# Query copies written once to DRAM by GpSimd, and loaded by one DMA per four heads

## The chip, the cores and the metric

The kernel runs on one core of one Trainium2 chip. The metric is device time in microseconds (us) of one execution, the median of several runs. Engines are named as in the profile: PE (TensorE matmul), PEld (TensorE weight load), DVE (VectorE), ACT (ScalarE), POOL (GpSimd) and SP (SyncE, whose queue, SPq, issues most DMAs).

## What is computed

Two transformer blocks over 2048 tokens of width 1024, batch 1, float32. The first (sliding-window attention, a gated recurrence, a mixture of experts) is not touched. The second has a chunked attention with relative positions, and beside it a sparse attention whose 256 keys per query are chosen by an index score. The change touches two inputs of that sparse branch, the queries `qb` (8 heads of 64) and the index queries `iq` (8 heads of 32):

```python
def second_block(x, norm_gain, w_in, ...):
    xn = rms_norm(h, norm_gain[layer])
    qa, ka, va, ga, qb, kb, vb, gb, iq, ik, iw, za, zb = jnp.split(xn @ w_in[layer], offsets, axis=-1)
    ya = chunked_relpos_attention(qa, ka, va, rel_bias[layer]) * jax.nn.silu(ga)
    qb, kb, iq, ik = (partial_rope(...) for each)          # 16 of 64 columns turn, 8 of 32 for the index
    yb = dsa_sparse_attention(qb, kb, vb, iq, ik, iw) * jax.nn.silu(gb)
    merged = gate_a * (ya @ w_branch_a) + gate_b * (yb @ w_branch_b)
    return rms_norm(h + merged @ w_out, final_norm_gain)

def one_block(blk):                                        # of dsa_sparse_attention, 128 queries
    logits = jax.nn.relu(jnp.einsum('bqhd,bsd->bqhs', iqb, ik))
    score = jnp.einsum('bqhs,bqh->bqs', logits, iwb)       # then masked by chunk
    _, idx = lax.top_k(score, 256)
    s = jnp.einsum('bqhd,bqkd->bqhk', qb, gather(k, idx)) * scale
    return jnp.einsum('bqhk,bqkd->bqhd', softmax(s), gather(v, idx))
```

## The kernel before

Tokens are cut into 16 blocks of 128. Float32 products are split: an operand is kept as a high and a low part of float32r, and products of parts are summed. For the sparse branch a head's query is needed with its columns repeated down the partitions (twice for `qb`, four times for `iq`), so that one matmul against the keys, which are stored with their high and low parts in different partitions, gives the whole product.

The second block, class `S3`, runs in stages. Each has front lanes, whose steps are asked first, and a back lane called `fill`, a chain of projections that is asked last:

1. Start: the norm of all 16 token blocks (`norm_lane`, for which POOL gathers two expert outputs of a block from DRAM, `cy<-Y`, and adds them, `cx`), and `proj(0, ...)`. Its token-row groups are numbered g: 0 is keys and values of the sparse branch, 1 is `iq`, 2 and 3 are `qb`, 4 and 5 are `va`. A group of one block is 24 matmuls into a `pA` bank.
2. `chunked(0)`: chunked attention (`a_unit`) of the first 8 blocks, and the selection (`sel_unit`) of blocks 2 to 7. The fill is the rest of the first half's projections, then the groups 0 to 5 and the transposed projections of the second half's blocks.
3. `sparse(range(10))`: sparse attention (`b_unit`) of blocks 0 to 9, beside what is left of that fill.
4. `chunked(1)`, with the selection of blocks 10 to 12, and the last projections as fill.
5. `sparse(range(10, 16))` with the output projections (`tail`) as fill.

The order on each engine is fixed when the program is built: lanes are generators, and a step is written when a clock model with a cost for each instruction (`Clock`, `Engine.cost`) says that its operands are near ready. Engines run their lists in order, so a step that is later on the chip than in the model holds what is behind it on its engine. A stage ends, and the next one's steps may be written, when this loop ends, so when no front lane and no spawned step is left (`ev_n` and others are spawned, by the fill too):

```python
while lanes or self.spawned:
```

Path of the queries: `ev_n` lets ACT copy a finished bank into a staging tile `st` (a ring of 3 tiles for all projections), POOL rotates it (`rotate`: six instructions) and stores it to the DRAM tensor `IQ` or `QB` by a DMA from its own queue. Later `turned` loads the queries of a block in two groups of four heads into the tile `x` (`x4`, one buffer): four DMAs on SP's queue per group, each reading one head's columns several times by a stride of zero. PE transposes the four parts, ACT and DVE split the result into `iqs` or `qd`. In all 28 groups of `IQ` and 32 of `QB` are loaded, 240 DMAs.

Of the kernel before, what the change touches and what calls it, by code (L numbers as in the profile page):

```python
# [16 lines left out]
AF = mybir.ActivationFunctionType  # L17
# [5 lines left out]
T = 2048  # L23
# [11 lines left out]
class Clock:  # L35
# [3 lines left out]
    def __init__(self):  # L39
        self.t = dict.fromkeys(("tensor", "vector", "scalar", "gpsimd", "sync", "dma"), 0.0)  # L40
        self.ready, self.last, self.by, self.free = {}, {}, {}, {}
        self.now, self.open = 0.0, set()
# [1084 lines left out]
class P2:  # L1127
# [184 lines left out]
    def put(self, dst, blk, t):  # L1312
        yield from self.b.load(dst[blk * 128:blk * 128 + 128, :], t)
# [544 lines left out]
class S3:  # L1858


    def __init__(self, b, X2, out, comb=None, skip=()):
        self.comb = comb
        self.b, self.nc, self.I, self.X2, self.out = b, b.nc, b.I, X2, out
        nc = b.nc
        dr = lambda n, s: None if n in skip else nc.dram_tensor(n, s, F32).ap()

        self.QA = dr("QA", (4, 4, 64, T))
        self.KA = dr("KA", (2, 4, 128, T))
        self.VA = dr("VA", (T, 1024))
        self.QB = dr("QB", (T, 512))  # L1870
        self.IQ = dr("IQ", (T, 256))
        self.SG = dr("SG", (8, 128, T))
        self.TZ = dr("TZ", (16, 128, T))
        self.YT = dr("YT", (8, 128, T))
        self.KEEP = dr("KEEP", (3, 128, T))
        self.XND = dr("XND", (2, 2, 128, KT, 512))

        self.parts = dr("W2P", (60, 2, 128, 1024))
        self.flags = set()

        self.with_tail = [i for i in range(24) if i % 3 < 2]
        self.exact, self.limit = False, 0
        self.xt = {}
        self.bias, self.stored = {}, set()
        self.BIAS = dr("BIAS", (NTB, 128, T))
# [174 lines left out]
    def ev_n(self, g, blk, ps):  # L2060
        b, nc = self.b, self.nc
        rp = self.rope[:, blk]
        r = slice(blk * 128, blk * 128 + 128)
        if g >= 4:
            v = yield from self.stage([128, 4, 2, 64], F32R)
            p4 = ps[:, 0:256].rearrange("p (h d) -> p h d", h=4)
            yield from b.on("scalar", ps, v)
            nc.scalar.activation(v[:, :, 0], p4, AF.Copy)
            yield 1
            yield from b.on("vector", v)  # L2070
            b.lo(v[:, :, 1], p4, v[:, :, 0])
            b.done(ps)
            yield 1
            yield from self.store(self.VA[r, (g - 4) * 512:(g - 4) * 512 + 512], v, v.rearrange("p h a d -> p (h a d)").bitcast(F32), ("va", blk, g - 4))
        elif g:
            h = 8 if g == 1 else 4
            x = yield from self.stage([128, h, 256 // h])
            yield from b.on("scalar", ps, x)
            nc.scalar.activation(x, ps[:, 0:256].rearrange("p (h d) -> p h d", h=h), AF.Copy)
            b.done(ps)  # L2080
            yield 1
            yield from b.on("gpsimd", x)
            if g == 1:
                self.rotate(x, rp[:, 16:20], rp[:, 20:24], 8, 4)
                dst, key = self.IQ[r, :], ("iq", blk)
            else:
                self.rotate(x, rp[:, 0:8], rp[:, 8:16], 4, 8)
                dst, key = self.QB[r, (g - 2) * 256:(g - 2) * 256 + 256], ("qb", blk, g - 2)
            yield 1
            yield from self.store(dst, x, x.rearrange("p h d -> p (h d)"), key, "gpsimd")  # L2090
        else:
            x = yield from self.stage([128, 424])
            yield from b.on("scalar", ps, x)
            nc.scalar.activation(x[:, 0:160], ps[:, 0:160], AF.Copy)
            nc.scalar.activation(self.iw[:, blk], ps[:, 160:168], AF.Copy, scale=1.0 / 16)
            b.done(ps)
            nc.scalar.activation(self.vbS[:, blk, 0], x[:, 64:128], AF.Copy)
            yield 1
            yield from b.on("vector", x)
            b.lo(self.vbS[:, blk, 1], x[:, 64:128], self.vbS[:, blk, 0])  # L2100
            yield 1
            yield from b.on("gpsimd", x)
            self.rotate(x[:, 0:64].unsqueeze(1), rp[:, 0:8], rp[:, 8:16], 1, 8)
            self.rotate(x[:, 128:160].unsqueeze(1), rp[:, 16:20], rp[:, 20:24], 1, 4)
            xx = x[:, 168:424].rearrange("p (i d) -> p i d", i=2)
            nc.gpsimd.tensor_copy(xx[:, 0].rearrange("p (a d) -> p a d", a=2), x[:, 0:64].unsqueeze(1).to_broadcast([128, 2, 64]))
            nc.gpsimd.tensor_copy(xx[:, 1].rearrange("p (a d) -> p a d", a=4), x[:, 128:160].unsqueeze(1).to_broadcast([128, 4, 32]))
            yield 1
            pt = yield from b.bank("pT")
            yield from b.on("tensor", xx, pt)  # L2110
            for i in range(2):
                nc.tensor.transpose(pt[:, i * 128:i * 128 + 128], xx[:, i], b.ident)
            b.done(x)
            yield 1
            kk, ii = self.kbS[:, r], self.ikS[:, r]
            yield from b.on("scalar", pt)
            nc.scalar.activation(kk, pt[:, 0:128], AF.Copy)
            nc.scalar.activation(ii, pt[:, 128:256], AF.Copy)
            yield 1
            yield from b.on("vector", kk)  # L2120
            b.lo(kk[64:128], pt[64:128, 0:128], kk[64:128])
            b.lo(ii[32:64], pt[32:64, 128:256], ii[32:64])
            b.lo(ii[96:128], pt[96:128, 128:256], ii[96:128])
            b.done(pt)
            self.flags.add(("kb", blk))
            yield 1
# [280 lines left out]
                    yield self.a_unit(p, c, t)  # L2407


    def turned(self, src, n, d, k, put):  # L2410

        b, nc, P = self.b, self.nc, self.P
        for g in range(n // 4):
            x = yield from P.get([128, 4, 128], F32, "x4", bufs=1)
            yield from b.on("sync", x)
            for h in range(4):
                c = (g * 4 + h) * d
                nc.sync.dma_start(x[:, h].rearrange("p (a d) -> p a d", a=k), src[:, c:c + d].unsqueeze(1).to_broadcast([128, k, d]))
            yield 1
            pt = yield from b.bank("pT")  # L2420
            yield from b.on("tensor", x, pt)
            for h in range(4):
                nc.tensor.transpose(pt[:, h * 128:h * 128 + 128], x[:, h], b.ident)
            b.done(x)
            yield 1
            yield from put(g, pt)
            b.done(pt)

    def sel_unit(self, blk):
        b, nc, P = self.b, self.nc, self.P  # L2430
# [11 lines left out]
        iq = yield from P.get([128, 8, 128], F32R, "iqs", bufs=1)  # L2442

        def put(g, pt):
# [5 lines left out]
            yield from b.on("vector", iq)  # L2450
            b.lo(o[64:128], p3[64:128], o[64:128])
            yield 1
        yield from self.turned(self.IQ[blk * 128:blk * 128 + 128, :], 8, 32, 4, put)
        acc = yield from P.get([128, self.NM], F32, "acc", bufs=self.nsel)
        pcs = [(a, min(N, a + 512)) for a in range(0, N, 512)]
        left = [0]
# [1 line left out]
        for j, (a0, a1) in enumerate(pcs):  # L2458
# [4 lines left out]
            for h in range(8):  # L2463
                ps = yield from b.bank("pS")
# [142 lines left out]
    def q_lane(self, blks):  # L2607
        b, nc, P = self.b, self.nc, self.P
        for blk in blks:
            yield from self.wait(("qb", blk, 0), ("qb", blk, 1))  # L2610
            qd = yield from P.get([128, 8, 2, 128], F32R, "qd", bufs=1)

            def put(g, pt):
                o = qd[:, g * 4:g * 4 + 4]
                p3 = pt.rearrange("p (h q) -> p h q", h=4)
                yield from b.on("scalar", pt, qd)
                nc.scalar.activation(o[:, :, 0], p3, AF.Copy)
                yield 1
                yield from b.on("vector", qd)
                b.lo(o[:, :, 1], p3, o[:, :, 0])  # L2620
                yield 1
            yield from self.turned(self.QB[blk * 128:blk * 128 + 128, :], 8, 64, 2, put)
            self.qd[blk] = qd

    def b_unit(self, blk, p):
# [472 lines left out]
```

## Time and profile before

| what | value |
|---|---|
| median of 3 runs (lowest, highest) | 4062.14 us (4050.82, 4066.87) |
| the profiled execution: its time, its span | 4061.26 us, 4059.4 us |
| granted TensorE clock, mean | 0.951 |
| PE, PEld busy | 3646.1 us (90%), 3167.4 us (78%) |
| DVE, ACT, POOL busy | 2734.8, 2283.2, 901.4 us (67, 56, 22%) |
| DMA packets; under 512 B | 425744; 129360 |

A busy time is a sum over the whole span; stages differ much in what limits them. The profiled execution is 0.88 us below the median of the runs.

### The profile page before, as it was taken

The page shows a single profiled execution, that of the slowest core. Times are in us where ns is not written, and L with a number is a line of the kernel's source. Part 1 is how long each engine was busy: PE and PEld are TensorE (multiplying, and loading weights), DVE is VectorE, ACT ScalarE, POOL GpSimd, SP SyncE. Part 2 cuts the span into 40 slices and gives each one's busy share as a digit, 9 for nine tenths or more (in the row PEclk, how much of TensorE's full clock was granted, in tenths as well). Part 3 has the DMA queues.
Part 4 walks back from the last instruction along what each step waited for, and adds up shares of the span by engine and source line. Part 5 has one row for each costly group of instructions (what it writes and reads, how often), then busy time and mean ns, then how long its engine had stood idle before and what let it go on. Part 6 is the DMA issues. An engine that isn't in the chain of part 4 may idle for free.

```text
span 4059.4 us, 64576 instructions
## 1 busy us (share of the span) xinstructions
PE 3646.1 (90%) x21649; PEld 3167.4 (78%) x21649; DVE 2734.8 (67%) x7027; ACT 2283.2 (56%) x4628; POOL 901.4 (22%) x1650
## 2 busy tenths in 40 slices
PE   3999999979969999397999989999889988999997
PEld 2888788768858888296777779888678877999997
DVE  7866785697777777526366743467766656878772
ACT  3654655565546666424257755357667774676751
POOL 1310000031011100473044526111033321211110
PEclk9999999979989999598999989999889998999999
DMA  6233451125358887739887773543166527787767
GB/s 229 79 108 110 137 198 60 64 81 167 130 202 314 314 315 285 263 126 339 290 255 249 249 283 108 169 147 101 43 187 180 173 81 270 259 281 272 265 230 283
DMA packets 425744, 801.28 MB, mean 197 GB/s; under 512 B 129360, under 2 KB 245296, under 8 KB 424496
## 3 DMA queue, kind: packets, MB, share of 16 engines
q1 hardware_dynamic: 407472, 748.70, 54.3%
q0 software_dynamic: 17920, 48.26, 3.5%
q8 instruction: 176, 2.88, 0.3%
q14 instruction: 176, 1.44, 0.1%
HBM read 571.02 MB, written 234.18 MB: 198 GB/s over the span
## 4 chain that ended last, share of the span: by engine, by line
PE 37%; DMA 7%; POOL 4%; DVE 3%; issue 3%; ACT 2%; SPq 1%; POOLq 0%; DVEq 0%; ACTq 0%
PE pA L122 22%; PE pS L122 5%; PE pT L122 5%; PE pU L122 5%; POOL rot L122 1%; DMA x<-IQ 1%; SPq L122 1%; DMA x<-QB 1%; DMA tz<-TZ 1%; POOL st L122 1%; DMA Q<-QA 0%; DMA sg<-SG 0%; DVE scb L122 0%; DVE pp L122 0%; POOL QB L122 0%
## 5 line engine op out<-in xcount | busy, mean ns | idle before, releaser
L122 PE MATMUL pA<-xnl,whi 128*128 128x512 f32 x1024 | 415.3, 406 | 5.4 <-DVE st L122 5.4
L122 DVE TENSOR_TENSOR wlo<-ld,whi 128x1024 fp32r<-128x1024 f32 x271 | 328.7, 1243 | 112.6 <-ACT whi L122 74.8
L122 PE MATMUL pA<-xnh,wlo 128*128 128x512 f32 x1024 | 403.7, 394 | 0.4 <-DVE wlo L122 0.4
L122 PE MATMUL pA<-xnh,whi 128*128 128x512 f32 x1024 | 403.9, 394 | 0.0
L122 DVE TENSOR_TENSOR pp<-pT,pp 128x256 fp32r<-128x256 f32 (+1 forms) x568 | 295.1, 537 | 117.5 <-ACT pp L122 113.8
L122 ACT ACTIVATE pp<-pT 128x256 fp32r<-128x256 f32 (+1 forms) x568 | 260.6, 478 | 201.5 <-PE pT L122 189.3
L122 PE MATMUL pA<-hlo,whi 128*128 128x512 f32 x832 | 352.1, 423 | 10.0 <-issue 6.7
L122 PE MATMUL pA<-hhi,wlo 128*128 128x512 f32 x832 | 328.8, 395 | 0.0
L122 PE MATMUL pA<-hhi,whi 128*128 128x512 f32 x832 | 327.9, 394 | 0.0
L122 ACT ACTIVATE whi<-ld 128x1024 fp32r<-128x1024 f32 x212 | 213.5, 1052 | 59.0 <-PE pA L122 35.3
L122 DVE SCALAR_TENSOR_TENSOR acc<-rl,iw,acc 128x512 f32<-128x512 f32 (+3 forms) x304 | 220.8, 727 | 38.0 <-ACT rl L122 31.4
L122 PEld LDWEIGHTS pA<-xnh,wlo 128*128 128x128 f32 x1024 | 193.9, 189 | 44.8 <-DVE wlo L122 1.1
L122 ACT ACTIVATE bias<-acc,sst 128x1152 f32<-128x1152 f32 (+13 forms) x168 | 220.0, 1309 | 13.3 <-DVE sst L122 9.6
L122 PEld LDWEIGHTS pA<-xnl,whi 128*128 128x128 f32 x1024 | 195.4, 191 | 33.6 <-issue 5.8
L122 PE MATMUL pA<-wlo,xnh 128*128 128x256 f32 (+1 forms) x672 | 200.9, 299 | 22.2 <-DVE st L122 12.4
L122 PEld LDWEIGHTS pA<-xnh,whi 128*128 128x128 f32 x1024 | 194.9, 190 | 29.4
L122 PE MATMUL pU<-pp,vbS 128*128 128x256 f32 x1088 | 203.2, 301 | 10.2 <-DVE pp L122 8.3
L122 ACT ACTIVATE rl<-pS 128x512 f32<-128x512 f32 (+3 forms) x304 | 163.6, 544 | 82.4 <-PE pS L122 42.9
L122 PE MATMUL pA<-whi,xnl 128*128 128x256 f32 (+1 forms) x672 | 197.5, 294 | 4.1 <-DMA xnl<-XND 4.1
L122 PE MATMUL pA<-whi,xnh 128*128 128x256 f32 (+1 forms) x672 | 197.6, 294 | 0.0
L122 ACT ACTIVATE st<-pA 128x256 f32<-128x256 f32 (+4 forms) x160 | 73.6, 460 | 202.6 <-PE pA L122 161.5
L122 PEld LDWEIGHTS pA<-hlo,whi 128*128 128x128 f32 x832 | 159.4, 192 | 35.9 <-issue 9.4
(494 smaller groups left out, 11117.2 us busy)
## 6 DMA issues: line engine op xcount, KB each, us to landing
whi<-W2P SPq DMA_DIRECT2D x172, 512.0 KB
wlo<-W2P SPq DMA_DIRECT2D x172, 512.0 KB
ld<-in_w_gu_dram SPq DMA_DIRECT2D x128, 512.0 KB
ld<-in_w_dn_dram SPq DMA_DIRECT2D x64, 512.0 KB
W2P<-whi SPq DMA_DIRECT2D x57, 512.0 KB
W2P<-wlo SPq DMA_DIRECT2D x57, 512.0 KB
Y<-ym SPq DMA_DIRECT2D x48, 512.0 KB
xl<-in_wadaT_dram SPq DMA_DIRECT2D x32, 512.0 KB
```

Source lines behind the costliest of these rows:

```text
L122: r = real(*a, **k)
```

## The change

The rotated queries get their copy in the staging tile: the tile is now `[128, h, 2, 256 // h]`, POOL copies the rotated half to the other half, and stores twice the width. `QB` and `IQ` have 1024 columns. A row of `QB` holds each head twice, stored by one DMA; a row of `IQ` holds each head four times, stored by two DMAs of the same tile, each in 1024 runs of 256 B. `turned` then loads 512 consecutive columns, that is four heads with all copies, by one DMA. Nothing else is edited.

```diff
-        self.QB = dr("QB", (T, 512))
-        self.IQ = dr("IQ", (T, 256))
+        self.QB = dr("QB", (T, 1024))
+        self.IQ = dr("IQ", (T, 1024))
...
             h = 8 if g == 1 else 4
-            x = yield from self.stage([128, h, 256 // h])
+            x = yield from self.stage([128, h, 2, 256 // h])
+            x0 = x[:, :, 0]
             yield from b.on("scalar", ps, x)
-            nc.scalar.activation(x, ps[:, 0:256].rearrange("p (h d) -> p h d", h=h), AF.Copy)
+            nc.scalar.activation(x0, ps[:, 0:256].rearrange("p (h d) -> p h d", h=h), AF.Copy)
...
-                self.rotate(x, rp[:, 16:20], rp[:, 20:24], 8, 4)
-                dst, key = self.IQ[r, :], ("iq", blk)
+                self.rotate(x0, rp[:, 16:20], rp[:, 20:24], 8, 4)
             else:
-                self.rotate(x, rp[:, 0:8], rp[:, 8:16], 4, 8)
-                dst, key = self.QB[r, (g - 2) * 256:(g - 2) * 256 + 256], ("qb", blk, g - 2)
-            yield 1
-            yield from self.store(dst, x, x.rearrange("p h d -> p (h d)"), key, "gpsimd")
+                self.rotate(x0, rp[:, 0:8], rp[:, 8:16], 4, 8)
+            nc.gpsimd.tensor_copy(x[:, :, 1], x0)
+            yield 1
+            if g == 1:
+                dst = self.IQ[r, :].rearrange("t (h b c) -> t h b c", h=8, b=2)
+                for i in range(2):
+                    yield from b.G("dma_start", dst[:, :, i], x.rearrange("p h a d -> p h (a d)"))
+                b.done(x)
+                self.flags.add(("iq", blk))
+            else:
+                yield from self.store(self.QB[r, (g - 2) * 512:(g - 2) * 512 + 512], x, x.rearrange("p h a d -> p (h a d)"), ("qb", blk, g - 2), "gpsimd")
...
-    def turned(self, src, n, d, k, put):
+    def turned(self, src, put):
...
-        for g in range(n // 4):
+        for g in range(2):
             x = yield from P.get([128, 4, 128], F32, "x4", bufs=1)
-            yield from b.on("sync", x)
-            for h in range(4):
-                c = (g * 4 + h) * d
-                nc.sync.dma_start(x[:, h].rearrange("p (a d) -> p a d", a=k), src[:, c:c + d].unsqueeze(1).to_broadcast([128, k, d]))
-            yield 1
+            yield from b.load(x.rearrange("p h d -> p (h d)"), src[:, g * 512:g * 512 + 512])
```

Since the clock model has a cost for the copies and stores, the built order changes from the first `iq` group on. Three places follow, in the order as built.

On POOL, at the first `iq` groups of the second half's blocks (in stage 2), each tile had its rotation and one store; before:

```order
L122 TENSOR_TENSOR rot<-st_27489,rope 128x32 x4
L122 TENSOR_TENSOR st_27489<-rot 128x8x4 x2
L122 DMA IQ<-st_27489 128x256
L122 TENSOR_TENSOR rot<-st_27543,rope 128x32 x4
L122 TENSOR_TENSOR st_27543<-rot 128x8x4 x2
L122 DMA IQ<-st_27543 128x256
```

And now:

```order
L122 TENSOR_TENSOR rot<-st_27443,rope 128x32 x4
L122 TENSOR_TENSOR st_27443<-rot 128x8x4 x2
L122 COPY st_27443<-st_27443 128x8x32
L122 DMA IQ<-st_27443 1024x1x64
L122 TENSOR_TENSOR rot<-st_27496,rope 128x32 x4
L122 TENSOR_TENSOR st_27496<-rot 128x8x4 x2
L122 COPY st_27496<-st_27496 128x8x32
L122 DMA IQ<-st_27443 1024x1x64
```

Each tile has one copy and one DMA more, and the next tile's rotation stands between its two stores.

On SP, where stage 3 begins (`x<-QB` is its first load, `BIAS<-bias` the last store of stage 2's selection); before:

```order
L122 DMA wlo_27772<-W2P 128x1024
L122 DMA BIAS<-bias_27457 128x1024
L122 DMA x_0_28016<-QB 128x2x64 x4
L122 DMA whi_28095<-W2P 128x1024
L122 DMA wlo_28096<-W2P 128x1024
L122 DMA whi_28101<-W2P 128x1024
L122 DMA wlo_28102<-W2P 128x1024
L122 DMA x_0_28121<-QB 128x2x64 x4
```

And now, nine rows after the store `BIAS<-bias_27640`:

```order
L122 DMA VA<-st_28429 128x512
L122 DMA VA<-st_28457 128x512
L122 DMA VA<-st_28504 128x512
L122 DMA x_0_28532<-QB 128x512
L122 DMA VA<-st_28546 128x512
L122 DMA VA<-st_28581 128x512
L122 DMA x_0_28599<-QB 128x512
```

The four loads are one, and the first load of stage 3 no longer follows that store: eight weight loads and three stores of group 4 (`VA`) have come between. Counted in PE's order, 312 matmuls of the fill (13 row groups of 24) that stood in stage 3 now stand before it. From the last fill matmul of stage 3 to its end there were 410 matmuls, now there are 572. Behind the end of stage 3 PE's two lists are nearly alike.

On POOL in stage 1, at the end of the first half's `qb` groups; before:

```order
L122 TENSOR_TENSOR rot<-st_20690,rope 128x32 x4
L122 TENSOR_TENSOR st_20690<-rot 128x4x8 x2
L122 DMA QB<-st_20690 128x256
L122 DMA cy_2_20297<-Y,pos 128x1024
L122 DMA cy_2_20793<-Y,pos 128x1024
```

And now, with 11 stores of `QB` still to come:

```order
L122 COPY st_20307<-st_20307 128x8x32
L122 DMA cy_2_20310<-Y,pos 128x1024
L122 DMA IQ<-st_20183 1024x1x64
L122 DMA cy_2_20388<-Y,pos 128x1024
L122 DMA IQ<-st_20261 1024x1x64
```

The gathers and the additions of two token blocks (8 and 9) have moved ahead of those stores.

## Rows read from the trace of the kernel before

**Rows 1.** Waits of PE from stage 2 on: us in total, times, longest.

```profile
PE pT L122 <- DMA x<-QB: 30.7, 8, 26.4
...
PE pT L122 <- DMA x<-IQ: 13.1, 17, 2.5
...
PE pS L122 <- DMA x<-IQ: 5.8, 1, 5.8
```

**Rows 2.** Timeline of SP and PE at the start of stage 5.

```profile
3352.22 2.41 SPq L122 DMA_DIRECT2D x<-QB  x4
...
3357.97 1.09 PE L122 MATMUL pT<-ident,x 128*128 128x128 f32 x4 [26.39 <-DMA x<-QB]
```

**Rows 3.** Stretches of stages 1 to 5: us, busy (and count) of each engine, clock, DMA.

```profile
1730.00:1830.00 100.00, 97.54 (x829) 97.33 (x828) 25.84 (x58) 28.62 (x79) 73.46 (x266) 1.00 0.38 133
1830.00:1920.00 90.00, 66.33 (x411) 61.86 (x411) 57.63 (x111) 39.39 (x75) 28.59 (x17) 0.85 0.93 337
...
2010.00:2500.00 490.00, 452.29 (x2492) 385.12 (x2491) 292.66 (x804) 307.98 (x772) 224.33 (x461) 0.97 0.74 238
```

**Rows 4.** Timeline of SP and PE around one `IQ` load (start, us).

```profile
2955.00 3.91 SPq L122 DMA_DIRECT2D x<-IQ  x4
...
2960.68 1.40 PE L122 MATMUL pS<-K,Q 128*128 128x320 f32 x4 [5.80 <-DMA x<-IQ]
...
2962.07 1.44 PE L122 MATMUL pT<-ident,x 128*128 128x128 f32 x4
```

**Rows 5.** Tiles x and IQ: duration ns min/median/max of issuing instructions; then landing.

```profile
L122 SPq DMA_DIRECT2D x<-QB x128: 359/468/1796, 2498.6 to 3869.2; - x128
L122 SPq DMA_DIRECT2D x<-IQ x112: 359/507/4374, 2017.1 to 3636.0; - x112
...
L122 POOL DMA_DIRECT2D IQ<-st x16: 580/580/630, 1726.7 to 2483.0; - x16
...
DMA to landing us min/median/max: 2.0/2.0/4.4
```

**Rows 6.** SP's issues (ns) of 1024 runs of 512 B, and of 128 rows.

```profile
L122 SPq DMA_DIRECT2D XND<-th x8: 519/520/1095, 1860.9 to 1946.0; - x8
L122 SPq DMA_DIRECT2D XND<-tl x8: 513/676/1465, 1866.0 to 1947.4; - x8
...
L122 SPq DMA_DIRECT2D KA<-st x32: 319/358/2719, 1908.9 to 2754.1; - x32
```

**Rows 7.** Timeline of POOL, one `iq` group of the second half, and the next one's begin.

```profile
2478.44 0.83 POOL L122 TENSOR_TENSOR rot<-st,rope 128x32 f32<-128x32 f32 x4 [0.64 <-ACT st L122]
2479.34 0.46 POOL L122 TENSOR_TENSOR st<-rot 128x32 f32<-128x32 f32 x2
2480.10 0.58 POOL L122 DMA_DIRECT2D IQ<-st  x1 [0.30 <-POOL st L122]
2481.32 0.82 POOL L122 TENSOR_TENSOR rot<-st,rope 128x32 f32<-128x32 f32 x4 [0.63 <-ACT st L122]
```

**Rows 8.** Groups by shape on POOL: copies, the gathers and their additions (busy, mean ns).

```profile
L122 POOL TENSOR_TENSOR cx<-cx,cy 128x1024 f32<-128x1024 f32 x16 | 44.8, 2800 | 83.8 <-DVE cy L122 74.6 <-DVE nrt L122 4.5 <-PE pT L122 4.2
L122 POOL DMA_INDIRECT cy<-Y,pos x32 | 36.0, 1126 | 65.7 <-DMA crow<-ROW 56.8 <-issue 6.4 <-POOL cx L122 1.5
...
L122 POOL COPY st<-st 128x128 f32<-128x128 f32 x32 | 8.8, 303 | 0.0
...
L122 POOL CAST VS<-c 128x256 fp32r<-128x256 f32 x1 | 0.4, 400 | 17.6 <-DMA ndist<-in_ndist_dram 17.6
```

**Rows 9.** Timeline of POOL in stage 1: stores of two blocks' `iq` groups.

```profile
1760.73 0.58 POOL L122 DMA_DIRECT2D IQ<-st  x1 [0.30 <-POOL st L122]
...
1769.35 0.58 POOL L122 DMA_DIRECT2D IQ<-st  x1 [0.30 <-POOL st L122]
```

**Rows 10.** Timeline of PE behind the gathers: three of its waits in stage 1.

```profile
1842.50 0.58 PE L122 MATMUL pA<-wlo,xnh 128*128 128x256 f32 x1 [4.11 <-DVE st L122]
1856.55 1.97 PE L122 MATMUL pT<-ident,cx 128*128 128x128 f32 x8 [5.33 <-DVE nrv L122]
1881.70 0.58 PE L122 MATMUL pA<-wlo,xnh 128*128 128x256 f32 x1 [5.16 <-DVE st L122]
```

**Rows 11.** Stretches of stage 3, with and without fill (columns as in rows 3).

```profile
2600.00:2700.00 100.00, 98.24 (x566) 84.35 (x565) 58.87 (x186) 43.60 (x98) 16.03 (x35) 1.00 0.55 164
...
2852.00:2900.00 48.00, 35.15 (x179) 26.89 (x178) 34.82 (x102) 35.69 (x68) 4.65 (x11) 0.86 0.11 38
2900.00:2950.00 50.00, 41.44 (x230) 32.43 (x230) 34.83 (x99) 25.70 (x43) 5.84 (x14) 0.86 0.16 43
```

More of the change, by code (lines that the diff above doesn't have):

```diff
@@ L2452, in put @@
             yield 1
-        yield from self.turned(self.IQ[blk * 128:blk * 128 + 128, :], 8, 32, 4, put)
+        yield from self.turned(self.IQ[blk * 128:blk * 128 + 128, :], put)
         acc = yield from P.get([128, self.NM], F32, "acc", bufs=self.nsel)
@@ L2621, in put @@
                 yield 1
-            yield from self.turned(self.QB[blk * 128:blk * 128 + 128, :], 8, 64, 2, put)
+            yield from self.turned(self.QB[blk * 128:blk * 128 + 128, :], put)
             self.qd[blk] = qd
```

## The prediction

> **What bounds the kernel now.** The page comes first: PE is busy for 90% of the span and everything else has room, so the change can win only where PE waits for something that it touches, and can lose wherever it makes PE wait. I then read PE's waits from stage 2 on, by what ended them [rows 1]. Loads of `x` end 30.7 + 13.1 + 5.8 = 49.6 us of them: the most that shorter loads could give back. The timeline at the start of stage 5 cuts that down [rows 2]: the longest wait, 26.4 us, ends with a load whose first DMA is issued at 3352.22, and PE starts at 3357.97. What held the load back until 3352.22 is the stage's end, so at most 5.8 us of the 26.4 belong to the load. Apart from it 49.6 − 26.4 = 23.2 us in 25 waits are left.
>
> Last, the stretches [rows 3]. From 1730 to 1830 PE is busy for 97.5 of 100 us and POOL for 73.5; from 1830 to 1920 PE has 66.3 of 90 at a clock of 0.85. From 2010 to 2500, where the fill makes the second half's `iq` and `qb`, PE has 452 of 490 and POOL 224. So POOL, idle by the average, is nearly full exactly where the change adds work.
>
> **The loads.** 240 DMAs become 60. Four issues of `IQ` hold SP for 3.91 us from 2955.00, and PE's first transpose of that group is at 2962.07, 7.1 us after the first issue [rows 4]. An issue costs SP about 0.47 (`QB`) or 0.51 us (`IQ`) [rows 5]; the new load moves 128 rows of 2 KB, and the nearest row, a DMA of 128 rows, takes 0.36 us [rows 6]. A median group thus gives back 4 × 0.49 − 0.36 = 1.6 us of issue, the example up to 3.5; about 2 us a wait is my reading. Of 25 waits (most far shorter than the longest, 2.5 and 5.8 us [rows 1]) with 23.2 us, mean 0.93, the shorter ones vanish and the longer ones keep part. All 23.2 can't go, since `x` has one buffer and each load still waits for the transposes before it. The upper end is 18 us, and 2 more at the stage-5 start; the lower end is 5, if what stands ahead of the load on SP is what is late. I take **−14**.
>
> SP is freed from 60 × 1.6 ≈ 100 us of issuing over all later stages, so weight loads and stores behind these loads start sooner. PE waits little for those: **−3** (0 to −8).
>
> **POOL in the second half.** One `iq` group of the fill takes 2.88 us from one rotation to the next (2478.44 to 2481.32), of which 0.64 us is idle [rows 7]; the work is 2.24. Added are a copy of 128×256, between the 0.30 us of a 128×128 copy and the 0.40 of a 128×256 cast [rows 8], so 0.4; and a second store. A store now costs 0.58 plus the 0.30 ahead of it [rows 7], 0.88. That is for 128 rows, and now there are 1024 runs. No row shows such a store from POOL, so I bound it. If runs are free: 2.24 + 0.4 + 0.88 = 3.52, or +0.64 over PE's 2.88, and for 8 blocks **+5**. If time goes by the run, a store takes 8 × 0.58 = 4.64, the group 2.24 − 0.88 + 0.4 + 2 × 4.94 = 11.6, +8.8 a block, **+71**. Between lies SP's row: 1024 runs of 512 B cost 0.52 to 0.68 against 0.36 for 128 rows [rows 6], a factor of about 1.6; with that a store is 0.93 and the group 4.22, +1.34 a block, +11. SP's row is nearest in shape, though on another engine; I take **+8**. That PE has no other work to put there follows from the fill: the groups stand in a row, and the front lane is asked first. The `qb` groups gain no DMA: 2.24 + 0.4 + 0.1 (wider store) = 2.75, below 2.88, hidden by the 0.64 us idle; without that cover each of 16 would cost 0.5.
>
> The Trainium skill has a rule on this (*DMA: Bandwidth & Descriptors*, "Anatomy of one DMA — SWDGE (gpsimd) path"): descriptor generation is a small, variable part, and "You can emit a lot of descriptors before the incremental cost shows up". By it the term would be at its lower end, 5 instead of 8. The trace can't say, since all POOL's direct stores in [rows 5] have 128 rows.
>
> **POOL in the first half (stage 1).** Where norm and projection mix, POOL has 100 − 73.5 = 26.5 us to spare per 100 us, and the stores of two blocks' `iq` groups are 8.62 us apart [rows 9]: 2.3 us to spare a block, and 1.3 to 2.0 are added: 0. Three `iq` groups that stand alone cost about 1 each, +3. Then the moved steps: the gathers of blocks 8 and 9, four of 1.13 us and an issue gap of 0.3 each, and two additions of 2.8 [rows 8], 11 us of POOL, now stand among the `QB` stores, where a group has 0.2 to spare. The ring of three tiles covers part: +5 (0 to +10). In return blocks 8 and 9 are ready earlier. Behind them PE waited 4.11, 5.33 and 5.16 us at a time [rows 10] while blocks came in late, in a stretch with a clock of 0.85 [rows 3]; two of eight blocks can earn about 6. Together **+2** (−10 to +12).
>
> **The fill moves.** 312 matmuls that stood in stage 3 now stand ahead of it, and the part of stage 3 without fill grows from 410 to 572 matmuls. From 2852 to 2950 PE was busy for 35.15 + 41.44 = 76.6 of 98 us, with 409 matmuls, at a clock of 0.86 [rows 11]: 0.240 us a matmul, 0.187 of it busy. With fill PE is 98% busy at full clock [rows 11], and the same busy time would be 0.187 × 0.86 = 0.161. So each of the 162 matmuls more without fill loses between 0.05 (idle alone) and 0.08 us (clock too), 8 to 13; I take **+11** (7 to 15).
>
> **The sum.** −14 − 3 + 8 + 2 + 11 = +4. The profiled execution took 4061.3; 4065.3, and with the 0.9 us by which the median of runs is higher, **4066 us**.
>
> **The rivals.** Within 0.5%, about 20 us, is about what a measurement of this kernel can tell from no change; my forecast lies in it with its bounds: −18 − 2 − 8 + 5 − 10 + 7 = −26 if all falls well, −5 + 0 + 11 + 12 + 15 = +33 if all falls badly. Chance **0.43** for 4042 to 4082.
>
> - *Faster: the loads give all they can, and POOL costs nothing.* −20 − 3, POOL's +5 and the tail's +7 taken up by other work of PE (a lane asked earlier), earlier norms −6: −29 to −20, about 4036. For it: 23.2 us of visible waits, 100 us less SP. Against it: the model hands the freed time to steps that [rows 3] show to be full. Chance 0.23.
> - *Slower: a store of POOL takes time by its runs.* It ends on the other side by one mechanism: 4061 − 17 + 11 + 71 in the second half, and 8 × (9.4 − 2.3) = 57 in the first, by 9.4 us added and 2.3 to spare: about 4183. It begins to decide, that is to take 20 us off the end, when a store holds POOL for over about 1.5 us. For it: no row of POOL's stores goes beyond 128 rows. Against it: SP's factor of 1.6 for 8 times the runs. Chance 0.11.
> - *Slower: the fill is short where it is needed.* With less fill in stage 3 the clock falls longer, and the `QB` stores delayed by 11 us of gathers hold `pA`, PE and all behind: the last two terms at twice their upper ends, 2 × (12 + 15) − 17 + 8 = +45, less what other waits absorb, about 4095. For it: the clock of 0.86 without fill. Chance 0.15.
> - *Slower: the stores of `IQ` land late.* A store now lands 2.0 us after issue [rows 5], in 1 KB rows. With 256-byte runs, and the DMA engines at 0.74 busy there [rows 3], the landing may take longer, and a tile of the ring of three is held for POOL's 3.5 us, ACT's copy of some 0.6, and the landing. Up to a landing of 3 × 3.52 − 4.1 = 6.5 us the ring covers it; at 10 us the pace is 14.1 / 3 = 4.7, or +1.2 over 3.52 for 16 `iq` groups: +19, about 4085. Chance 0.08. The Trainium skill speaks for this one (*DMA: Bandwidth & Descriptors*, "Specifications"): below 512 B a transfer falls short of line rate, since the engine reads, modifies and writes; that no store of the profile lands slower than 4.4 us [rows 5] is no evidence, since `IQ` had rows of 1 KB.
>
> **Range and chances.** Most of the first rival and the two slower ones near 4090 belong into it, the 4183 stays out: 4032 to 4105, with some 0.8. Faster by over 0.5%: 0.23; within: 0.43; slower: 0.11 + 0.15 + 0.08 = 0.34.
>
> **What would show it.** Loads: 60 of `x`, about 0.36 us each on SP, and PE's waits for them below 10 us apart from a stage's start; if 15 or more stay, SP's issue was not what was late. POOL: the duration of its 32 stores of `IQ`: 0.58 means +5, 0.9 means +11, 4.6 the second rival; between two rotations of the second half's `iq` groups 3.5 to 4.2 us, with PE's waits for `pA` beside them. Landing of these stores under 6.5 us, or the last rival. Stage 1: gathers earlier, waits like those of [rows 10] fewer, and new ones for `pA` among the `qb` groups. Fill: the first load of `QB` later than 2499, and a stretch without fill of some 130 us at a clock below 0.9 at the end of stage 3. What would make the forecast wrong first is the one price that nothing shows, the store in 1024 runs.

## The result and the profile after

The changed kernel takes 4107.34 us (median of 4 runs, 4105.39 to 4111.34) against 4059.81 us for the kernel before: a ratio of 1.012, interval 1.0097 to 1.0142. It is slower by some 47 us, where I had forecast 4066 us and no difference that can be told.

First PE's waits from stage 2 on, as in [rows 1] (us in total, times, longest):

```profile
PE pT L122 <- DMA x<-QB: 38.8, 9, 31.9
...
PE pA L122 <- ACT st L122: 10.9, 5, 3.0
...
PE pT L122 <- DMA x<-IQ: 9.0, 8, 3.9
```

By these rows the waits for `x` are 47.8 us in place of 49.6. But 5.8 of the 49.6 were never waits for `x`: that row is the first `pS<-K,Q` of stage 4, a matmul that does not read `x`. The same matmul waits as long in the changed kernel, and there the profile names a load of `Q`:

```profile
PE pS L122 <- DMA Q<-QA: 5.7, 1, 5.7
```

Like for like the waits are 47.8 us in place of 43.8, and without the wait at the start of stage 5 (31.9, before 26.4) 15.9 in place of 17.4. A new wait stands beside them: PE waits for a bank that ACT has not yet copied into a staging tile.

The issues and landings of the changed kernel, as in [rows 5], first of the tile `x`, then of the tensor `IQ`:

```profile
L122 SPq DMA_DIRECT2D x<-QB x32: 319/376/738, 2574.1 to 3913.5; - x32
L122 SPq DMA_DIRECT2D x<-IQ x28: 319/366/1587, 2039.0 to 3678.3; - x28
...
DMA to landing us min/median/max: 2.7/4.5/10.4
```

```profile
L122 POOL DMA_DIRECT2D IQ<-st x32: 834/872/972, 1732.5 to 2522.5; - x32
...
  ACT st L122: 13.8, 6
```

An issue of the load costs 0.37 us, as forecast, but the load lands 4.5 us later. A store in 1024 runs holds POOL for 0.87 us, between the flat price (0.58) and SP's ratio (0.93), and ACT waits 13.8 us for such stores to land.

The stretches that answer to [rows 3] and [rows 11] (us, busy and count of PE, PEld, DVE, ACT, POOL, clock, DMA):

```profile
1730.00:1830.00 100.00, 83.27 (x650) 80.66 (x650) 35.85 (x79) 29.78 (x83) 81.34 (x241) 0.93 0.50 179
1830.00:1920.00 90.00, 70.45 (x495) 68.76 (x494) 40.83 (x79) 31.27 (x60) 43.80 (x75) 0.86 0.81 286
2010.00:2500.00 490.00, 460.48 (x2456) 394.08 (x2454) 294.13 (x800) 301.22 (x750) 214.35 (x429) 0.95 0.74 247
2850.00:2900.00 50.00, 35.88 (x197) 28.74 (x195) 36.00 (x100) 47.47 (x96) 5.48 (x14) 0.91 0.16 55
2900.00:2950.00 50.00, 38.41 (x190) 30.10 (x190) 36.14 (x103) 37.75 (x72) 5.34 (x12) 0.81 0.07 22
2950.00:3000.00 50.00, 37.29 (x230) 28.95 (x230) 34.93 (x102) 25.37 (x43) 6.34 (x14) 0.97 0.27 76
```

From 1730 to 1830 PE is busy for 83 us, where it was busy for 97.5. The first load of `IQ` is issued at 2039.0, where it was at 2017.1 [rows 5]: it comes 22 us later, and 20 of these are lost in stage 1 (the table of stages below). The part of stage 3 without fill now runs from 2857 to 3002, at clocks of 0.81 to 0.97.

What PE's waits in stage 1 consist of, in the timelines of ACT and POOL (start, us):

```profile
1804.31 1.15 ACT L122 ACTIVATE cy<-cy,wts 128x1024 f32<-128x1024 f32 x1 [7.05 <-DMA cy<-Y,pos]
1806.24 0.38 ACT L122 ACTIVATE st<-pA 128x256 f32<-128x256 f32 x1 [0.78 <-DMA IQ<-st]
```

```profile
1797.26 1.11 POOL L122 DMA_INDIRECT cy<-Y,pos  x1 [0.35 <-issue]
1798.37 0.92 POOL L122 DMA_DIRECT2D IQ<-st  x1
1799.60 1.07 POOL L122 DMA_INDIRECT cy<-Y,pos  x1 [0.30 <-issue]
1800.66 0.91 POOL L122 DMA_DIRECT2D IQ<-st  x1
```

ACT waits 7.05 us for a moved gather, which stands behind stores on POOL. The staging copy is behind it in ACT's list and then waits 0.78 us more for a store of `IQ`; PE starts again at 1806.67, after 8.90 us:

```profile
1806.67 0.58 PE L122 MATMUL pA<-wlox,xnh 128*128 128x256 f32 x1 [8.90 <-ACT st L122]
```

At the `iq` groups of stage 2 the timeline of ACT shows another thing:

```profile
2498.09 0.36 ACT L122 ACTIVATE st<-pA 128x256 f32<-128x256 f32 x1
...
2499.09 1.15 ACT L122 ACTIVATE bias<-acc,sst 128x1024 f32<-128x1024 f32 x1
...
2501.11 1.15 ACT L122 ACTIVATE bias<-acc,sst 128x1024 f32<-128x1024 f32 x1
...
2503.13 1.15 ACT L122 ACTIVATE bias<-acc,sst 128x1024 f32<-128x1024 f32 x1
...
2505.02 0.36 ACT L122 ACTIVATE st<-pA 128x256 f32<-128x256 f32 x1
```

Three steps of the selection's search (2.0 us each with what belongs to them) stand between two staging copies, so this group takes 6.9 us where [rows 7] show 2.88. No store is what is late here: ACT's list was written so. The clock model charges POOL 0.69 us for a copy and 1.04 for each store; that it took POOL for the bound there is my reading of it.

### The profile page after: what moved, and what is told of

It reads as the page before. It is cut to its first block, busy times and chain, and to the rows that moved or that the text cites. A ratio compares the mean times of both kernels' runs of the same rounds, so it can differ in the third digit from the quotient of the medians.

```text
span 4103.6 us, 64431 instructions
## 1 busy us (share of the span) xinstructions
PE 3658.7 (89%) x21649; PEld 3180.9 (78%) x21649; DVE 2736.2 (67%) x7027; ACT 2284.4 (56%) x4628; POOL 933.8 (23%) x1714
## 3 DMA queue, kind: packets, MB, share of 16 engines
q8 instruction: 176, 2.88, 0.3%
## 5 line engine op out<-in xcount | busy, mean ns | idle before, releaser
L122 PE MATMUL pA<-wlo,xnh 128*128 128x256 f32 (+1 forms) x672 | 209.8, 312 | 49.2 <-ACT st L122 20.1
L122 ACT ACTIVATE bias<-acc,sst 128x384 f32<-128x384 f32 (+13 forms) x168 | 220.1, 1310 | 10.8 <-DVE sst L122 6.9
L122 PE MATMUL pS<-kbS,qd 128*128 128x512 f32 (+3 forms) x640 | 177.5, 383 | 12.1 <-DVE bst L122 11.8
```

Source lines behind the costliest of these rows:

```text
L122: r = real(*a, **k)
```

## The experiments

Two theories stood at first: the loss is paid on the chip by POOL's added **work**, or by the **order** that the model's charges make. A third, that the loads give nothing, was looked at beside them. `b.clock.op` charges the clock model; `nc.gpsimd.eng` issues an instruction that the model doesn't see. Ratios are to the kernel before, run on the same chip.

| run | median us | ratio (95% interval) |
|---|---|---|
| e1 load alone, own order | 4062.22 | 1.0001 (0.9988 to 1.0013) |
| e2 stores alone, four loads | 4117.33 | 1.0127 (1.0108 to 1.0146) |
| e3 work, not charged | 4096.53 | 1.0078 (1.0060 to 1.0096) |
| e4 charges, no work | 4102.50 | 1.0094 (1.0076 to 1.0113) |
| e5 IQ twice, one store | 4104.06 | 1.0109 (1.0089 to 1.0128) |
| e6 gathers behind | 4116.56 | 1.0128 (1.0105 to 1.0152) |
| e7 QB only | 4103.02 | 1.0102 (1.0083 to 1.0122) |
| f1 load alone, order of before | 4034.79 | 0.9931 (0.9912 to 0.9949) |
| f2 all work, order of before | 4062.87 | 1.0003 (0.9987 to 1.0019) |
| f3 charge of 0.69 only | 4105.75 | 1.0106 (1.0080 to 1.0131) |
| f4 charge of 0.02 only | 4097.25 | 1.0082 (1.0057 to 1.0107) |
| g1 IQ twice, order of before | 4051.54 | 0.9972 (0.9959 to 0.9986) |
| g2 QB only, order of before | 4064.45 | 1.0000 (0.9985 to 1.0015) |
| g3 two loads per QB group | 4067.28 | 1.0016 (1.0001 to 1.0031) |
| g4 charge of 0.40 only | 4097.58 | 1.0088 (1.0059 to 1.0117) |
| h1 second store from SP | 4047.33 | 0.9964 (0.9951 to 0.9977) |
| h2 half and half | 4054.39 | 0.9992 (0.9981 to 1.0003) |

**e1 to e4: parts of the change, in the orders that they make.** e1, on the kernel before (the threshold of the exact fallback is raised too, so that wrong queries don't start it):

```diff
+            n = src.shape[1]
+            yield from b.load(x.rearrange("p h d -> p (h d)").rearrange("p (a c) -> p a c", c=n), src.unsqueeze(1).to_broadcast([128, 512 // n, n]))
```

> Stores, rotation and tensors are those of before; only the loads change: one load per four heads, of 512 columns as they lie (all of a row of QB, a row of IQ twice). So the heads in x are not the right ones; the selection and the sparse attention run on wrong queries. GpSimd's work and what the clock model charges for it are as before, and the built order differs from that of before only from the first load of stage 3 on. If the shorter load gives what I forecast for it (17 us): 4043. If a load's landing and the queue ahead of it are what PE waits for, and not the number of issues: 4055 to 4062. If one load changes the order for the worse by itself: over 4070.

> Copies and stores of the changed kernel, but four loads per group again, each 128 columns. If the single load gives nothing: 4107 as the changed kernel. If it gave my 14 to 17 us: 4121 to 4124.

e3 issues copy and stores unseen by the model, which is charged once:

```diff
+            nc.gpsimd.eng.tensor_copy(x[:, :, 1], x0)
...
+            b.clock.op("gpsimd", [dst], [x], 1.04, 0.0, 0.364)
```

> The changed kernel's work (copies, two stores of 1024 runs, one load), but the clock model is charged for one store of 0.364 us of transfer as before and for no copy, so that the built order is that of the load-alone run until stage 4. If the added work on the chip costs the time (POOL time and tiles held until the stores land): 4095 to 4110, and in stage 1 and at the end of stage 2 PE waits for staging copies as in the changed kernel. If the order that the model's charges make costs it: the time of the load-alone run within 8 us, about 4060 to 4068.

> The load-alone kernel, but the clock model is charged for the copy and the second store as in the changed kernel, with no such instruction: the order of the changed kernel until stage 3, without its added work; like the load-alone run it computes on wrong queries. If the order costs the time: 4095 to 4110, with the first load of IQ near 2039 as in the changed kernel. If the work costs it: 4055 to 4065, with the first load of IQ near 2017.

The load alone gives nothing in its own order, work without charges costs 34 us, and charges without work cost 40: both theories seemed to hold half. e2 lies between its two forecasts. Its lists are those of the changed kernel row for row up to 3916 us, and there four loads of 512 B runs cost more than the one load, by 3 us of the ratios (1.0127 against 1.012) or 10 of the medians, which is not clear of noise. The profiles showed why these runs could not decide. The lists of e3 and of e1 part in stage 4, those of e4 and of the changed kernel in stage 3, and behind these places the stages differ by up to 20 us although no work differs (stage 5 takes 725.7 us in e4 and 704.9 in the changed kernel).

**e5 to e7: parts of the work, in their own orders.**

> As the changed kernel, but a row of IQ holds each head twice (512 columns), stored by one DMA of 128 rows; two loads per group write the copies of x. The copy stays, the second store and the 1024 runs are gone; the built order of stages 1 and 2 has the shape of before again (gathers behind all stores of QB, eight IQ groups in a row). If the second store of IQ, by its charge in the model and its time on the chip, makes most of the loss: 4062 to 4072. If the copies and the wider QB stores make it: over 4085.

> As the changed kernel, but the norm lane waits with block 8 until the last store of QB of the first half is written, so that no gather stands among the stores; nothing else is held. If the moved gathers cost the half of stage 1's loss that the order makes: 9 to 11 us less than the changed kernel up to the first load of IQ, and 4093 to 4100 in all. If early norms are a gain: over 4107.

> Only QB is changed (copy, wider store, one load per group); IQ is stored once and loaded by four DMAs as before. If IQ's stores make the loss: 4058 to 4070, with no wait of PE for a staging copy of over 2 us in stage 1. If copies on GpSimd by themselves cost, half of the loss stays: about 4085.

None of the three came out as I had thought likeliest. e5 and e6 lie in the second range that I had named, but the causes named with these ranges do not hold: g1 below has e5's copies and wider stores and is faster than the kernel before, and e6 loses nothing in stage 1, where the early norms were. e7 lies in neither of its ranges. QB alone, with little work on POOL and no 1024 runs, costs 41 us; in its first stage nothing is lost (337.6 us, 342.1 before), but the front of stage 2 (the stretches are those of the table below), the rest of stages 2 and 3, and stages 4 and 5 are longer by 10, 16, 9 and 9. Gathers put back in their place bring stage 1 only 3 us, and the whole is no faster than the changed kernel. So the loss was not where I had seen it, at `IQ` and the gathers; the order was under suspicion everywhere.

**f1 to f4 and g4: order and work apart.** f1 and f2 keep the lists of before on PE and DVE row for row, since the one load is charged as four (the lines of f2):

```diff
+            nc.sync.eng.dma_start(x.rearrange("p h d -> p (h d)"), src[:, g * 512:g * 512 + 512])
+            for h in range(4):
+                b.clock.op("sync", [x[:, h]], [src], 128 * 128 * 4 / 3.6e5)
```

f3, f4 and g4 are the kernel before with a charge for no work (0.69 us for `QB` groups, 0.02 and 0.40 for both kinds; each also tells the model that the tile is ready 0.1 us later):

```diff
+            b.clock.op("gpsimd", [x], [x], 0.02, 0.1)
```

> The load-alone kernel (it computes on wrong queries), with the one load charged in the clock model as four: every engine's list is that of before, row for row, but for the loads. So its time is the price of the load and of nothing else. By my forecast of the load: 4045. If PE's waits for x come from landing and from the place of the load in SP's list: 4056 to 4062. If the built order gave the loss in the other runs, the waits for x fall here by some us and nothing else moves.

> All that the changed kernel does (copies, two stores of IQ, wider store of QB, one load), charged in the clock model as before: PE's and DVE's lists are those of before, row for row. Theory one, that GpSimd's added work and the held staging tiles cost the 46 us: 4090 or more. Theory two, that the work costs about 10 to 20 us in stage 1 and at the IQ groups of stage 2, and the rest is the built order: 4070 to 4080. Theory three, that nearly all is the order: 4055 to 4066.

> The kernel before, nothing added or removed; only the clock model is charged 0.69 us of GpSimd for each QB group, as for the copy that is not there. If the built order of before is a lucky one that any new charge leaves: 4080 to 4105, as the run with QB alone. If that run lost by its work: 4062 within 10.

> The kernel before with a charge of only 0.02 us of GpSimd for each IQ and QB group, which stands for nothing. If small shifts of the model alone reorder the lists at a price: 4075 to 4100; if only the large charges matter: 4062 within 10.

> The kernel before, nothing added; the clock model is charged 0.40 us of GpSimd for each IQ and QB group. If a new order has its price whatever the charge: 4085 to 4110, as with 0.02 and 0.69. If the two others were unlucky: 4062 within 10.

This parts order from work. With the order of before the loads give 4061.2 − 4034.8 = 26 us, the whole change costs 1.7 us, and so POOL's work takes 28 us back. The order, not the work, is the 44 us between f2 and the changed kernel, which do the same work. A charge that stands for nothing costs 36 (0.02), 35 (0.40) and 45 us (0.69), so a new order can cost as much without any work. In every pair of runs with the same work on the chip, the one in a new order is the slower, by 28 to 66 us when taken from the ratios: e1 and e4 against f1, e3, e6 and the changed kernel against f2, e5 against g1, e7 against g2, and f3, f4 and g4 against before.

By stages, from one profile each (marks: the first transpose of `cx`, the first load of `IQ`, the first issue of the last load of `IQ` ahead of the first of `QB`, the first `pS<-K,Q` of stage 4, the first load of `QB` in stage 5, the end):

| us | stage 1 | front of 2 | rest of 2, 3 | 4 | 5 |
|---|---|---|---|---|---|
| before | 342.1 | 370.1 | 573.5 | 391.5 | 707.2 |
| f1 load alone | 340.4 | 356.0 | 569.4 | 392.7 | 699.9 |
| f2 all work | 355.0 | 357.9 | 580.5 | 388.1 | 700.1 |
| g1 IQ twice | 341.9 | 367.0 | 573.9 | 388.6 | 707.4 |
| h1 second store SP | 342.8 | 359.0 | 574.9 | 389.3 | 706.5 |
| after | 361.9 | 360.1 | 602.7 | 396.8 | 704.9 |

These are single executions; those of h1 and g1 took 12 and 9 us more than the medians of their runs, so a figure of the table can be off by some us.

What the order does between f2 and the changed kernel can be read from PE. From the start of stage 1 its idle time is 254 us in place of 224, and its busy time, for the same matmuls, 2172 in place of 2158. Of the waits, the one that grows most is for a staging copy by ACT (in f2, then in the changed kernel, from 1640 on):

```profile
PE pA L122 <- ACT st L122: 5.6, 3, 2.4
```

```profile
PE pA L122 <- ACT st L122: 29.0, 12, 8.9
```

In e4, the changed kernel's charges without its work, this wait is 20.4 us. In f3, f4 and g4 it is 1.0 us at most: those orders lose about as much, but at other places.

One row of PE's waits from stage 2 on in the kernel before, and then those of f1:

```profile
PE pT L122 <- POOL sc L122: 15.8, 10, 4.1
```

```profile
PE pT L122 <- DMA x<-QB: 32.0, 7, 26.9
PE pT L122 <- POOL sc L122: 10.6, 10, 3.8
PE pT L122 <- DMA x<-IQ: 10.0, 8, 3.3
```

The loads gain 14 of their us in the front of stage 2 and 7 in stage 5, but the waits for `x` are less by only 43.8 − 42.0 = 1.8 us over all stages. f2 and h1, which compute the right result, show the gain in the front of stage 2 too (357.9 and 359.0). There PE is idle for 15.4 us in place of 23.2; 5.2 of these 7.8 us come from a wait for POOL in the chunked attention, to which no `x` belongs. The other 6.2 us are shorter busy time of PE, with the clock at half for 7 us of that stretch in place of 14. What links the loads to either is not shown.

**g1 to g3, h1, h2: which work, which loads.**

> Order of before, charged as before. A row of IQ holds each head twice, stored once in 128 rows; two loads per IQ group; QB as in the changed kernel. The copies stay, the second store and the 1024 runs are gone. If the second store of IQ makes most of GpSimd's 28 us: 4036 to 4045, faster than both kernels. If the copies and wider stores make it: 4052 to 4062.

> Order of before, charged as before. Only QB has copies, a wider store and one load per group; IQ is as before. In stage 2 before the first load of QB nothing of the loads is changed. If the load gain there (14 us in the load-alone run) comes from IQ's loads, it is gone here and 12 us are left: 4048 to 4060 with the work of the QB groups hidden. If the gain comes from QB's loads: 4036 to 4045.

> Order of before, tensors and stores of before. A group of QB is loaded by two DMAs, one for each copy, in place of four; IQ by four as before. No work of GpSimd is added. Half of the QB loads' issues go: if the number of issues makes the gain, half of QB's 12 us, 4054 to 4058; if the short runs of 256 B make it, 4060 as before.

h1 is f2 but for the engine that issues the second store:

```diff
-                    nc.gpsimd.eng.dma_start(d4[:, :, 1], src)
+                    nc.sync.eng.dma_start(d4[:, :, 1], src)
```

> As the run with all work in the order of before, but the second store of an IQ tile is issued by SP. GpSimd then holds one store per tile. If GpSimd's time for the second store (0.9 us each) took stage 1's 14 us: stage 1 falls back to about 345 us and the kernel to 4045 to 4050. If the tile held until the stores land took it: as before the move, 4060. If SP, waiting for the rotation, keeps loads behind it: over 4065.

> Order of before. IQ of blocks 0 to 7 is stored twice by one DMA and loaded by two, IQ of blocks 8 to 15 as in the changed kernel; QB as in the changed kernel. Stage 1 should be as in the run with IQ twice (342 us), the front of stage 2 too (367), the later stages as in the run with all work: 4045 to 4050. If the second store's price in stage 2 outweighs the one load: 4055 or more.

The loads of `QB` give nothing that can be measured: g2 has them with the copies that they need, g3 has two of them without copies (its four loads per group of `IQ` are cut by copy in place of by head, so it is not a clean run). Those of `IQ` are left to make the gain. g1 has all copies and the wider `QB` stores, and stage 1 is as before: the copies are hidden there. f2 and h1 differ in who issues the second store, and in stage 1 by 12 us. In f2, in the timeline of POOL, then in ACT's waits from 1730 to 1850:

```profile
1796.55 1.76 POOL L2097 DMA_DIRECT2D IQ<-st  x2 [0.30 <-POOL st L2089]
...
1800.45 1.74 POOL L2097 DMA_DIRECT2D IQ<-st  x2 [0.30 <-POOL st L2089]
...
1804.33 1.74 POOL L2097 DMA_DIRECT2D IQ<-st  x2 [0.30 <-POOL st L2089]
```

```profile
ACT st L122 <- DMA IQ<-st: 19.7, 5, 7.0
```

and the same wait in h1:

```profile
ACT st L122 <- DMA IQ<-st: 9.6, 3, 4.4
```

A lone `iq` group takes 3.9 us in f2 (1796.55 to 1800.45, and so on), where the same groups are 2.6 to 3.3 us apart before, and staging tiles are held on top of it until both stores have landed. But that is the smaller part. PE's lists in f1 and f2 are the same, so the lag of f2 can be followed matmul by matmul. It is 0.7 us up to this wait, for a tile that POOL rotates (ACT had waited 4.5 us for a store of `IQ` to put a copy into the ring):

```profile
1776.01 0.56 PE L122 MATMUL pT<-ident,st 128*128 128x128 f32 x2 [1.31 <-POOL st L122]
```

Then it is 2.2, and without a further wait it grows to 8.8 us by 1790, because the granted clock falls to the lower of its two levels (1.2 GHz) from 1776.9 to 1790.5. The same stretch in f2 and in f1 (columns as in [rows 3]):

```profile
1780.00:1790.00 10.00, 10.00 (x48) 10.00 (x48) 1.72 (x3) 2.24 (x7) 9.07 (x41) 0.50 0.37 127
```

```profile
1780.00:1790.00 10.00, 10.00 (x87) 10.00 (x87) 4.34 (x9) 3.81 (x11) 8.61 (x35) 1.00 0.68 229
```

The lone `iq` groups add 2.4 us, the `qb` groups behind them the rest. Whether the clock falls there in every execution of f2 is not shown. With the second store off POOL's queue the clock stays at its upper level there, and stage 1 takes 342.8 us, 2.4 more than in f1. h1 doesn't tell POOL's time from the time that a tile is held, since its second store is also issued earlier. h1, which leaves nothing out, is faster than both kernels at 4047.3 us; g1 is next. h2, which joins g1's first half to f2's second, came between its two forecasts, and its gain cannot be told from none.

## Why the prediction was wrong

**The step that failed is "The fill moves"**. The prediction prices a new order by the steps that can be seen to move, 312 matmuls in this term and the gathers of two blocks in the term for stage 1, and puts all other differences of the lists at nothing, without a reason. I priced the reordering at +11 us in stage 3 and at nothing net in stage 1. It cost 44 us, 7 in stage 1, 2 in the front of stage 2, 22 in the rest of stages 2 and 3, 9 in stage 4 and 5 in stage 5 (after against f2), though I had called PE's lists behind stage 3 nearly alike. The +11 itself was right: from the last fill matmul to stage 4 it took 144.8 us, against 106.2 before, and 38.6 less 162 × 0.161 = 26 is 12.5. What I left out is the rest of the new lists. Of the 45 us between the two profiles 31 are idle time of PE, and the wait for ACT's staging copies alone grew by 23 us (29.0 against 5.6), at copies that stand behind a late gather or behind three steps of the search. The other 14 us are longer busy time, which I can't assign to places. Every other order that was tried cost 28 to 66 us for the same work, with the loss at different places. So the order of before is better than all those tried beside it; why, and whether a search over charges found it, was not shown.

**The loads** were mis-sized, −17 against −26 (0.9931, interval 0.9912 to 0.9949), and for a wrong reason. I took the gain from the waits for `x`. Of their 49.6 us 5.8 belonged to a load of `Q`, so 17.4 us in 24 waits were to be had apart from stage 5's start, not 23.2 in 25; and in f1 the waits fell by 1.8 us only. 15.1 us of them stay, which by the sign that the prediction set (15 or more) says that SP's issue was not what was late. The gain is in `IQ`'s loads, most of it while the chunked attention runs. What frees it there, SP's time or the short runs, stays open: g3 halves only the issues of `QB`, e2, with four loads and longer runs, is not clear of noise against the changed kernel, and no run has the short runs in that order.

**POOL in the second half** was close: +8 forecast; f2 against f1 shows 11 in the rest of stages 2 and 3, and the store's 0.87 us is near SP's ratio. (The upper bound of 71 is 8 × 8.8 = 70, and POOL, busy for 224 of 490 us, was not nearly full there.) The Trainium skill (*DMA: Bandwidth & Descriptors*, "Anatomy of one DMA — SWDGE (gpsimd) path") calls descriptor generation a small, variable part; the trace agrees, 0.29 us more for eight times the runs, and the rival that a store takes time by its runs fell.

**POOL in the first half** was mis-sized: +2 with the moved gathers, 15 by f2 against f1, where no gather has moved. The +3 for the three `iq` groups that stand alone was about right (2.4). What failed is the 0 for the groups where norm and projection mix, whose slack was an average over 100 us: there a tile held until its stores had landed stopped ACT, PE waited 1.3 us for POOL, and the lower clock behind it cost another 6.6. I had counted POOL's work there and no clock. The tile held until the landing is the mechanism of the last rival, at landings mostly below the 6.5 us that it asked for (2.8 to 7.1 us in f2's stage 1). The Trainium skill's "Specifications" on the same page (transfers below 512 B fall short) points the same way, but weakly: an undisturbed store of `IQ` lands after 2.8 us, against 2.3 for the same bytes in 128 rows (g1), and 0.29 of the difference is POOL's issue.

**The rivals.** The third, a fill short of supply and banks held in stage 1, named two of the places and came nearest with 4095; it too saw only the moved places. The first priced loads that give all they can and a POOL that costs nothing at 4036; f1, which has no work of POOL, lies at 4035. That is luck in part: the rival's sum has earlier norms for −6, and f1, in the order of before, has none.

## What to carry to other kernels

Where a model sets the order at build time, time a charge for no work first: it tells how much an edit can seem to cost by the new order alone, here 35 to 45 us. Then measure an edit in the old order, by charging the model as before, and only then let the order follow. Slack of an engine, averaged over a stretch, does not show that added work is free there: in f2 PE's wait of 1.3 us for POOL, in a stretch with 26% of POOL free before, stood ahead of 13.6 us at half clock.

## What the runs showed that I had not expected

- A charge of 0.02 us per group in the clock model (and 0.1 us until the tile is ready), with the same instructions, moved the kernel by 36 us (1.0082).
- One load for four saves SP three issues, some 1.5 us a group, but little of that reaches the landing. From the first issue of a group to the landing of its last DMA, in the median, `QB` takes 4.5 to 4.8 us with four loads (f3, f4, g4; the trace of the kernel before has no landings of `x`) and 4.5 to 5.2 with one (f1, f2, after); `IQ` takes 5.5 to 5.9 with four and 4.8 with one.
- SP's issue of a store in 1024 runs of 256 B takes 0.52 us (h1), POOL's 0.87.
